# SSD decay differences of three heads: from a broadcast load and VectorE arithmetic to TensorE products of block-diagonal operands

## The chip, the cores and the metric

The kernel runs on one core of one Trainium2 chip. The metric is the device time of one execution in microseconds (us), lower is better. The engines are called as the profile calls them: PE is TensorE (matmul), PEld its weight load, DVE is VectorE, ACT is ScalarE, POOL is GpSimd, SP is SyncE, which only issues transfers here. ACT and POOL issue some transfers as well.

## The reference

The program is a two-layer backbone over 512 latent and 256 context tokens of 1024 channels. What the change touches is the chunked state-space mixer (SSD) of layer 0. It has 24 heads in 4 groups of 6, two directions, and chunks of 128 tokens: 6 chunks in all, 2 of them context.

```python
acs = jnp.cumsum(chunks(dt * a), axis=2)
seg = acs[:, :, :, None] - acs[:, :, None, :]
decay = jnp.exp(jnp.where(mask, seg, -jnp.inf))
cb = jnp.einsum('bclgn,bcsgn->bclsg', cm_c, bm_c)
y_diag = jnp.einsum('bclsgh,bcsghp->bclghp', cb[..., None] * decay, xdt)
```

For each chunk and head, `seg[l, s]` is the difference of two running sums, one at the token `l` that is written and one at the token `s` that is read. It is needed for both directions, where it is clamped so that the exponent is never positive.

## The kernel before, in words

The program is one long list of instructions, which a scheduler puts into an order for each engine ahead of time; each engine then runs its own list strictly in that order and waits on semaphores. A transfer also takes one of eight completion semaphores (DMAHW0 to DMAHW7) in turn for SP and ACT together, so a transfer whose semaphore is still in use waits for the one eight places earlier.

**Start (lines 596 to 628).** SP loads x and the modulation weights `mraw` (512 KB each, tiles reused), PE sums them (L580), and DVE copies the sum out (L587). Nothing of the first projections runs before that.

**Time steps (dt_stage, lines 659 to 711).** The running sums `acs` of 6 chunks x 48 head-directions are made on PE (L693), transposed (L707), copied to `at` by ACT (L709) and written by one transfer to the DRAM table `acd` (L710). Meanwhile the Fourier channels go on: `dft_channels` leaves its product in PSUM, ACT casts it to `ah` and DVE forms the rest `al` (L96, L97, shown as `ah`, `al`), and `dft_tokens` multiplies these on PE (L123).

**SSD (lines 796 to 1116).** For each of 4 groups, `ssd(G)` yields step by step, and between its steps the main loop emits filling work: `xbc_unit` (projection, a 5-tap convolution `co` on DVE at L855), `z_block`, and for the last group the output projection (`accumulate1`, L480). Splitting a weight into two parts takes ACT (L96) and DVE (L97). `decay(G, c, a)` is called 48 times, for 4 groups, 6 chunks and the two halves `a` of three heads. At the first half it forms `cb2` (L913, L915). Then SP loads `ab`, the sums of three heads in two directions broadcast to all 128 partitions (L918). DVE subtracts the sum at `s` (`nacs`) and clamps, three times for one direction (L924) and three times for the other, taking the minimum of both (L926). ACT and DVE form the weighted `w` (L923, L929), ACT takes the exponent (L932), POOL multiplies (L933), and `diag` uses the result one step later (L941).

The ring `ab` has two buffers, so the load of one call waits for the exponent of the call two before. PSUM has eight banks: four for `ps_mm` (ps1: the large products), two for `ps_s` (psum1: states, cb, transposes), one each for `ps_y` and `ps_off`.

Of the kernel before, what the change touches and what calls it, by code (L numbers as in the profile page):

```python
# [8 lines left out]
F32 = mybir.dt.float32  # L9
F32R = mybir.dt.float32r  # L10
# [16 lines left out]
FILL_LEAD = 1.0  # L27
LAMBDA_INIT = 0.8 - 0.6 * math.exp(-0.3)
# [27 lines left out]
def backbone_kernel(ctx, tc, xt, vec, dtrow, dskip, lam, w_mod, w_gate, w_up, w_down, w_in0, w_out0, w_in1, w_out1,  # L56
                    consts, dft_c, dft_l, rope, out):
# [88 lines left out]
    # ------------------------------------------------------------ modulation vectors  # L146
# [68 lines left out]
    def step_after(gen, n, after):  # L215
        """Steps of background work that no engine issues before the given instructions."""
        with ExitStack() as st:
            for i in after:
                st.enter_context(tc.issue_after(i))
            step(gen, n)  # L220
# [5 lines left out]
    # ------------------------------------------------------------ norms over channels  # L226
# [5 lines left out]
    def rsqrt(y, src, count):  # L232
        """1 / sqrt(src / count + eps): Newton's iteration from a guess that halves the exponent."""
# [84 lines left out]
    def gate(t, src, g):  # L318
        """The channels that GpSimd takes, scaled ahead of the rest"""
# [3 lines left out]
    def scale_both(t, src, g, r, a=0, b=KT):  # L323
        """t = src, scaled by channel and by token, from channel tile a to b; t holds the gated channels already"""
# [5 lines left out]
    def shift_split(t, m, xh, xl):  # L330
        """The two parts of t, shifted by channel"""
# [10 lines left out]
    def hasty(f):  # L342
        """Puts a stage of the turn before what is emitted ahead of it but doesn't wait for it."""
# [5 lines left out]
    class Turn:  # L349
        """Residual update of h by the mixer or FFN output o, then the next pre-norm, in stages per token block."""  # L350
# [32 lines left out]
        def last(self, b, psum1, between, out):  # L383
            """The whole update of the last block: nothing else is left to hide its steps."""
# [48 lines left out]
        def whole(self):  # L433
            """The pre-norm, put together again from its parts"""
# [5 lines left out]
    class Shift:  # L440
        """A tile of one token block, addressed by the tokens of the whole."""
# [7 lines left out]
    class Blocks:  # L449
        """Token blocks kept apart, addressed by the tokens of the whole."""  # L450
# [31 lines left out]
    # ------------------------------------------------------------ layer 0  # L482
# [5 lines left out]
    acd = dram.tile([6, 48, 128], F32, name="acd")  # L488
# [5 lines left out]
    nacs = sd.tile([128, 6, 48], F32, name="nacs")  # L494
# [8 lines left out]
    # time steps of the SSD and Fourier channels  # L503
    with ExitStack() as es:
# [38 lines left out]
        def scaled(b):  # L543
            """The pre-norm scaled, without its shift."""
# [114 lines left out]
        def dt_stage():  # L659
# [38 lines left out]
            nc.scalar.mul(nacs, acs, -1.0)  # L698
# [1267 lines left out]
```

## Time and profile before

| what | value |
|---|---|
| runs, us | 2404.7, 2405.3, 2398.96; median 2404.7 |
| span of the profiled execution, us | 2404.4 (the page gives no other time for it) |
| PE busy | 2123.5 us (88%) |
| DVE busy | 1951.7 us (81%) |
| ACT busy | 1124.8 us (47%) |
| POOL busy | 1187.3 us (49%) |
| mean granted PE clock | 0.934 of full speed |

Busy time counts the time from an instruction's start to its end; matmuls are pipelined, so a busy PE is not necessarily at its peak rate. The chain of waits is followed back from the last instruction: each step names what released it. A group of the trace's lines gives busy time and the mean of one, then the idle time of the engine before it and what ended that idle time.

### The profile page before, as it was taken

The page shows a single profiled execution, that of the slowest core. Times are in us where ns is not written, and L with a number is a line of the kernel's source. Part 1 is how long each engine was busy: PE and PEld are TensorE (multiplying, and loading weights), DVE is VectorE, ACT ScalarE, POOL GpSimd, SP SyncE. Part 2 cuts the span into 40 slices and gives each one's busy share as a digit, 9 for nine tenths or more (in the row PEclk, how much of TensorE's full clock was granted, in tenths as well). Part 3 has the DMA queues.
Part 4 walks back from the last instruction along what each step waited for, and adds up shares of the span by engine and source line. Part 5 has one row for each costly group of instructions (what it writes and reads, how often), then busy time and mean ns, then how long its engine had stood idle before and what let it go on. Part 6 is the DMA issues. An engine that isn't in the chain of part 4 may idle for free.

```text
span 2404.4 us, 33829 instructions
## 1 busy us (share of the span) xinstructions
PE 2123.5 (88%) x12594; PEld 1888.4 (79%) x12594; DVE 1951.7 (81%) x3035; ACT 1124.8 (47%) x1966; POOL 1187.3 (49%) x903
## 2 busy tenths in 40 slices
PE   7898989888987779899999987988889977999997
PEld 3787878776767678889999987766667776899997
DVE  4858987879897788998888878788778777888886
ACT  4535565646433344333333443654556643544443
POOL 1525656556543546664555543284842223555553
PEclk9999999999998689999999988998889987999998
DMA  7334332324430523333333321111101213222321
GB/s 257 132 130 137 124 112 81 129 89 147 139 113 7 165 100 110 114 114 132 120 118 133 124 97 53 44 44 36 42 29 40 75 44 114 79 106 98 105 97 53
DMA packets 90390, 239.43 MB, mean 100 GB/s; under 512 B 8433, under 2 KB 38289, under 8 KB 90225
## 3 DMA queue, kind: packets, MB, share of 16 engines
q1 hardware_dynamic: 71808, 214.95, 26.1%
q10 hardware_dynamic: 16944, 17.20, 2.2%
q0 software_dynamic: 1472, 5.11, 0.5%
q8 instruction: 99, 1.62, 0.3%
q14 instruction: 67, 0.54, 0.1%
HBM read 217.82 MB, written 18.37 MB: 98 GB/s over the span
## 4 chain that ended last, share of the span: by engine, by line
PE 41%; DVE 35%; issue 7%; DMA 7%; ACT 6%; POOL 4%; SPq 0%; ACTq 0%; POOLq 0%; DVEq 0%
PE ps_mm L123 33%; DVE w L97 6%; DMA mraw<-in_w_mod_dram 4%; DVE w L929 2%; DVE macc L175 2%; DVE co L855 2%; DMA ab<-acd 2%; DVE ab L924 2%; DVE ab L926 1%; PE ps_at L123 1%; DVE sx L1518 1%; DVE facc L326 1%; DVE mx L1629 1%; PE ps_s L580 1%; POOL wt L1184 1%
## 5 line engine op out<-in xcount | busy, mean ns | idle before, releaser
L123 PE MATMUL ps_mm<-xh,w 128*128 128x256 f32 (+2 forms) x3600 | 854.5, 331 | 55.6 <-DVE w L97 20.3
L123 PEld LDWEIGHTS ps_mm<-xh,w 128*128 128x128 f32 x3600 | 616.8, 197 | 108.3 <-DVE w L97 24.2
L123 PE MATMUL ps_mm<-xl,w 128*128 128x256 f32 (+2 forms) x1800 | 557.6, 329 | 8.6 <-DVE xl L338 3.5
L123 PE MATMUL ps_mm<-hid,w 128*128 128x384 f32 (+2 forms) x2244 | 408.0, 339 | 30.8 <-DVE facc L1371 11.9
L123 PEld LDWEIGHTS ps_mm<-hid,w 128*128 128x128 f32 x2244 | 367.5, 193 | 62.8 <-DVE facc L1371 17.6
L123 PEld LDWEIGHTS ps_mm<-xl,w 128*128 128x128 f32 x1800 | 339.1, 196 | 31.8 <-DVE xl L338 4.1
L97 DVE TENSOR_TENSOR w<-raw,w 128x512 fp32r<-128x512 f32 (+1 forms) x292 | 312.1, 1076 | 35.5 <-ACT w L96 34.3
L96 ACT CAST w<-raw 128x512 fp32r<-128x512 f32 (+1 forms) x323 | 236.9, 749 | 149.2 <-PE ps_mm L123 128.4
L180 POOL TENSOR_TENSOR macc<-macc,mraw 128x1024 f32<-128x1024 f32 x54 | 152.8, 2829 | 121.5 <-ACT mraw L179 118.0
L97 DVE TENSOR_TENSOR w<-wt,w 128x512 fp32r<-128x512 f32 x156 | 159.0, 1028 | 39.3 <-ACT w L96 39.2
L123 PE MATMUL ps_mm<-ys,w 128*128 128x256 f32 (+1 forms) x840 | 161.2, 348 | 22.1 <-ACT ys L96 8.9
L123 PEld LDWEIGHTS ps_mm<-ys,w 128*128 128x128 f32 x840 | 131.6, 201 | 43.9 <-DVE acc L480 12.3
L1184 POOL TENSOR_TENSOR wt<-raw 128x512 f32<-128x512 f32 x78 | 118.3, 1516 | 55.1 <-DMA raw<-in_w_up_dram 40.7
L96 ACT CAST w<-wt 128x512 fp32r<-128x512 f32 x156 | 93.4, 618 | 101.7 <-PE ps_mm L123 53.8
L1371 DVE TENSOR_TENSOR facc<-facc,ps_mm 128x384 f32<-128x384 f32 (+2 forms) x232 | 119.2, 557 | 21.1 <-PE ps_mm L123 20.9
L123 PE MATMUL ps_mm<-w,xh 128*128 128x256 f32 x576 | 118.6, 305 | 12.9 <-ACT cin L849 10.7
L97 POOL TENSOR_TENSOR w<-raw,w 128x1024 fp32r<-128x1024 f32 x31 | 81.1, 2615 | 82.5 <-ACT w L96 82.4
L175 DVE SCALAR_TENSOR_TENSOR macc<-mraw,silc,macc 128x1024 f32<-128x1024 f32 x54 | 98.3, 1820 | 27.4 <-DMA mraw<-in_w_mod_dram 27.2
L1184 POOL TENSOR_TENSOR wt<-raw,wt 128x512 f32<-128x512 f32 x39 | 64.6, 1656 | 104.0 <-DVE w L97 103.3
L123 PEld LDWEIGHTS ps_mm<-w,xh 128*128 128x128 f32 x576 | 96.1, 202 | 19.0 <-ACT cin L849 12.7
L179 ACT ACTIVATE mraw<-mraw,silc 128x1024 f32<-128x1024 f32 x54 | 62.1, 1152 | 84.4 <-DVE macc L175 35.8
L1516 POOL TENSOR_TENSOR sx<-sx 128x512 f32<-128x512 f32 x60 | 95.3, 1588 | 2.3
(405 smaller groups left out, 4273.7 us busy)
## 6 DMA issues: line engine op xcount, KB each, us to landing
mraw<-in_w_mod_dram SPq DMA_DIRECT2D x96, 512.0 KB, 4.2
raw<-in_w_in_dram SPq DMA_DIRECT2D x69, 512.0 KB, 3.4
raw<-in_w_gate_dram SPq DMA_DIRECT2D x44, 512.0 KB, 3.3
raw<-in_w_up_dram SPq DMA_DIRECT2D x44, 512.0 KB, 3.2
raw<-in_w_down_dram SPq DMA_DIRECT2D x44, 512.0 KB, 3.3
ab<-acd SPq DMA_DIRECT2D x48, 384.0 KB, 3.7
raw<-in_w_out_dram SPq DMA_DIRECT2D x32, 512.0 KB, 3.3
res<-rd ACTq DMA_DIRECT2D x5, 1024.0 KB, 8.7
```

The costliest lines, as they stand in the source:

```text
L96: nc.scalar.copy(hi, raw)
L97: (eng or nc.vector).tensor_tensor(out=lo, in0=raw, in1=f32(hi), op=SUB)
L123: last = nc.tensor.matmul(dst, a, b[:, sl], start=(start and i == 0), stop=(stop and i == 2))
L175: nc.vector.scalar_tensor_tensor(out=acc, in0=raw, scalar=s, in1=acc, op0=MUL, op1=ADD)
L179: nc.scalar.activation(raw, raw, AF.Identity, scale=s)
L180: nc.gpsimd.tensor_tensor(out=acc, in0=acc, in1=raw, op=ADD)
L855: nc.vector.scalar_tensor_tensor(out=co, in0=cin[:, j:j + CW], scalar=vcol(V_CW5 + ti * 5 + j), in1=co, op0=MUL, op1=ADD)
L924: nc.vector.tensor_scalar(out=ab[:, 0, h, :], in0=ab[:, 0, h, :], scalar1=nacs[:, c, r0 + h:r0 + h + 1], scalar2=0.0, op0=ADD, op1=ALU.min)
L929: nc.vector.scalar_tensor_tensor(out=w[:, h, :], in0=G.cb2[:, 1], scalar=dtt[:, c, r0 + 3 + h:r0 + 4 + h], in1=w[:, h, :], op0=MUL, op1=ADD)
L1184: nc.gpsimd.tensor_tensor(out=t, in0=a, in1=b, op=op)
L1371: nc.vector.tensor_tensor(out=acc[:, m, s], in0=acc[:, m, s], in1=ps, op=ADD)
L1516: nc.gpsimd.tensor_tensor(out=cv, in0=cv, in1=t, op=ADD)
```

## The change

The table `acd` gives way to `sgd`, one block of 24 rows by 896 columns for each chunk and each three heads. Rows 0 to 11 hold the sums along `l` in block-diagonal places (12 rows: high and low part of three heads in two directions) over a weight of -1; rows 12 to 23 hold ones in block-diagonal places over the sums along `s` as weights. The constant part comes from the input `segbg` by one DRAM-to-DRAM transfer with a broadcast source, issued on ACT at the start; the sums are written into it by 32 small transfers on ACT in `dt_stage`. In `decay`, SP loads one block into one of two fixed tiles `sg`, two PE products of 384 columns leave minus the difference of both directions in PSUM, ACT writes the positive part (Relu) to `ex`, DVE takes one maximum over 128x384, and ACT takes the exponent of the negative. The bank count goes from 4 and 2 to 3 and 3. Comments removed by the diff are left out here.

```diff
+SG_R, SG_N = 24, 896
...
-    acd = dram.tile([6, 48, 128], F32, name="acd")
+    sgd = dram.tile([6, 8, SG_R * SG_N], F32, name="sgd")
+    nc.scalar.dma_start(out=sgd.rearrange("c a n -> (c a) n"),
+                        in_=segbg.rearrange("r n -> (r n)").partition_broadcast(48))
...
-            nc.scalar.mul(nacs, acs, -1.0)
...
-            at = tp.tile([48, T], F32, tag="at", name="at")
-            nc.scalar.copy(at, pq[0:48, :])
-            nc.scalar.dma_start(out=acd.rearrange("c h t -> h c t"), in_=at.rearrange("h (c t) -> h c t", c=6))
+            at = [p.tile([48, T], F32R, tag=t, name="at", bufs=1) for p, t in ((tp, "at"), (fp, "yo"))]
+            split(pq[0:48, :], *at)
+            for i, p in enumerate(at):
+                p = f32(p)
+                for a in range(8):
+                    src = p[6 * a:6 * a + 6].rearrange("j (c t) -> j c t", c=6)
+                    r0 = 6 * i * SG_N
+                    nc.scalar.dma_start(
+                        out=sgd[:, a, r0:r0 + 6 * 1024].rearrange("c (j m) -> j c m", m=1024)[:, :, 0:128], in_=src)
+                    r0 = (12 + 6 * i) * SG_N
+                    nc.scalar.dma_start(
+                        out=sgd[:, a, r0:r0 + 6 * SG_N].rearrange("c (j m) -> j c m", m=SG_N)[:, :, 768:SG_N], in_=src)
...
         def ps1():
-            return psp.tile([128, 512], F32, tag="mm", name="ps_mm", bufs=4)
+            return psp.tile([128, 512], F32, tag="mm", name="ps_mm", bufs=3)
         def psum1():
-            return psp.tile([128, 512], F32, tag="s", name="ps_s", bufs=2)
+            return psp.tile([128, 512], F32, tag="s", name="ps_s", bufs=3)
...
-            ab = sq_.tile([128, 2, 3, 128], F32, tag="ab", name="ab", bufs=2)
-            nc.sync.dma_start(out=ab.rearrange("p d h l -> p (d h) l"),
-                              in_=acd[c, r0:r0 + 6, :].partition_broadcast(128))
+            sg = state["sg"][state["n"] % 2]
+            state["n"] += 1
+            nc.sync.dma_start(out=f32(sg[0:SG_R, :]), in_=sgd[c, 2 * g + a].rearrange("(r n) -> r n", n=SG_N))
+            pds = []
+            for d in range(2):
+                pd = psum1()[:, 0:GW]
+                nc.tensor.matmul(pd, sg[:, 768:SG_N], sg[:, d * GW:d * GW + GW], start=True, stop=True)
+                pds.append(pd.rearrange("p (h l) -> p h l", h=3))
+            ex = sq_.tile([128, 3, 128], F32, tag="ex", name="ex", bufs=3)
+            nc.scalar.activation(ex, pds[0], AF.Relu)
             w = sq_.tile([128, 3, 128], F32, tag="w", name="w", bufs=2)
-            ex = sq_.tile([128, 3, 128], F32, tag="ex", name="ex", bufs=3)
             for h in range(3):
                 nc.scalar.activation(w[:, h, :], G.cb2[:, 0], AF.Identity, scale=dtt[:, c, r0 + h:r0 + h + 1])
-                nc.vector.tensor_scalar(out=ab[:, 0, h, :], in0=ab[:, 0, h, :],
-                                        scalar1=nacs[:, c, r0 + h:r0 + h + 1], scalar2=0.0, op0=ADD, op1=ALU.min)
-                nc.vector.scalar_tensor_tensor(out=ab[:, 0, h, :], in0=ab[:, 1, h, :],
-                                               scalar=nacs[:, c, r0 + 3 + h:r0 + 4 + h], in1=ab[:, 0, h, :],
-                                               op0=ADD, op1=ALU.min)
                 nc.vector.scalar_tensor_tensor(out=w[:, h, :], in0=G.cb2[:, 1],
                                                scalar=dtt[:, c, r0 + 3 + h:r0 + 4 + h], in1=w[:, h, :],
                                                op0=MUL, op1=ADD)
-            nc.scalar.activation(ex, ab[:, 0], AF.Exp)
+            nc.vector.tensor_tensor(out=ex, in0=ex, in1=pds[1], op=ALU.max)
+            nc.scalar.activation(ex, ex, AF.Exp, scale=-1.0)
             nc.gpsimd.tensor_tensor(out=ex, in0=ex, in1=w, op=MUL)
...
-        state = {}
+        state = {"n": 0, "sg": [sq_.tile([128, SG_N], F32R, name="sg%d" % i) for i in range(2)]}
+        for sg in state["sg"]:
+            nc.gpsimd.memset(f32(sg), 0.0)
```

The change's own file has other line numbers: there the broadcast transfer is L490, the 32 transfers are L717 and L720, `cb2` is L926, the two products are L935, the Relu is L938, `w` on DVE is L942 and the maximum is L945.

The order of the instructions moves at three places. The first is SP at the start of the program: x, the modulation weights and the first weights of layer 0. The names in brackets are what a row waits for. Before:

```order
L75 DMA vecs<-in_vec_dram 128x445
L528 DMA x_111<-in_xt_dram 128x8x256
L576 DMA mraw<-in_w_mod_dram 128x1024 x3
L576 DMA mraw<-in_w_mod_dram 128x1024 [waits DMAHW0_49]
L576 DMA mraw<-in_w_mod_dram 128x1024 [waits DMAHW1_49]
L576 DMA mraw<-in_w_mod_dram 128x1024 [waits DMAHW4_49,DMAHW2_49,PE_49]
L107 DMA raw<-in_w_in_dram 128x1024 [waits DMAHW3_49]
```

And with the change:

```order
L76 DMA vecs<-in_vec_dram 128x445
L530 DMA x_111<-in_xt_dram 128x8x256
L578 DMA mraw<-in_w_mod_dram 128x1024 x2
L578 DMA mraw<-in_w_mod_dram 128x1024 [waits DMAHW0_49]
L578 DMA mraw<-in_w_mod_dram 128x1024 [waits DMAHW1_49]
L578 DMA mraw<-in_w_mod_dram 128x1024 [waits DMAHW2_49]
L578 DMA mraw<-in_w_mod_dram 128x1024 [waits DMAHW4_49,DMAHW3_49,PE_49]
```

The broadcast transfer on ACT has taken a completion semaphore. The other early transfers hold 0 (consts), 1 (vecs), 2 (x), 4 and 6 (mraw), 5 (dsk) and 7 (rows), so it holds DMAHW3, and the sixth `mraw` now waits for it.

The second place is ACT while the time steps end and the third Fourier group is cast (`ah`). Before, one transfer stands between the casts:

```order
L709 COPY at<-ps_mm 48x768 [waits PE_49]
L96 CAST ah<-ps_s 128x512 [waits PE_49,Activation_49]
L710 DMA acd<-at 48x6x128 [waits Activation_49]
L703 ACTIVATE tend<-tend 128x288 [waits DVE_49]
L96 CAST ah<-ps_s 128x512 [waits PE_49] x2
```

With the change 32 transfers stand there. The last ones and what follows them:

```order
L720 DMA sgd<-at 6x6x128 [waits DMAHW5_49]
L717 DMA sgd<-at 6x6x128 [waits DMAHW6_49]
L720 DMA sgd<-at 6x6x128 [waits DMAHW7_49]
L717 DMA sgd<-at 6x6x128 [waits DMAHW0_49]
L720 DMA sgd<-at 6x6x128 [waits DMAHW1_49]
L97 CAST ah<-ps_s 128x512 [waits PE_49] x2
```

The second and third cast of that group have moved behind all 32 transfers; PE's own order in this stretch is unchanged.

The third place is the decay itself in the first group of the SSD. On DVE, before, from the third `cb` on:

```order
L915 TENSOR_TENSOR cb_2498<-ps_s,cs 128x256 [waits PE_49]
L924 TENSOR_SCALAR ab<-ab,nacs 128x128 [waits DMAHW2_49,Activation_49]
L924 TENSOR_SCALAR ab<-ab,nacs 128x128
L855 SCALAR_TENSOR_TENSOR co<-cin,vecs,co 128x772 [waits DVE_49]
L924 TENSOR_SCALAR ab<-ab,nacs 128x128
L926 SCALAR_TENSOR_TENSOR ab<-ab,nacs 128x128 [waits DVE_49] x2
L929 SCALAR_TENSOR_TENSOR w<-cb_2498,dtt,w 128x128 [waits Activation_49]
```

On DVE with the change, from the same `cb` on:

```order
L926 TENSOR_TENSOR cb_2530<-ps_s,cs 128x256 [waits PE_49]
L942 SCALAR_TENSOR_TENSOR w<-cb_2530,dtt,w 128x128 [waits Activation_49] x6
L945 TENSOR_TENSOR ex<-ex,ps_s 128x384 [waits PE_49,Activation_49]
L971 TENSOR_TENSOR t<-ps_off,eac 128x192 [waits PE_49]
L971 TENSOR_TENSOR t<-ps_off,eac 128x192
```

On PE with the change, where one of the new products stands among those of a projection:

```order
L124 MATMUL ps_mm<-xh_74,w 128x256
L124 MATMUL ps_mm<-xl_75,w 128x512
L124 MATMUL ps_mm<-xl_75,w 128x256
L124 MATMUL ps_mm<-xh_74,w 128x512
L124 MATMUL ps_mm<-xh_74,w 128x256
L935 MATMUL ps_s<-sg_2112 128x384 [waits DMAHW2_49,DVE_49]
```

The load's wait has moved from DVE, where L924 had it, to PE, where L935 has it together with a wait for a free bank.

## Rows read from the trace of the kernel before

**Rows 1.** The page's head.

```profile
span 2404.4 us, 33829 instructions
```

**Rows 2.** Busy time and clock in the stretch 240 to 740 us (the SSD).

```profile
core 0: us, PE busy (x) PEld busy (x) DVE busy (x) ACT busy (x) POOL busy (x), PEclk, DMA share, GB/s
240.00:740.00 500.00, 447.34 (x2625) 382.01 (x2624) 422.12 (x830) 263.93 (x486) 281.01 (x347) 0.96 0.34 113
```

**Rows 3.** The chain of waits by line, 240 to 740 us.

```profile
by line: PE ps_mm L123 25.5%; DVE w L929 9.3%; DMA ab<-acd 7.9%; issue 7.6%; DVE ab L924 7.4%; DVE ab L926 6.3%; DVE co L855 5.1%; PE ps_s L894 3.6%; DVE w L97 3.2%; DVE bc L855 3.1%; DVE acc L480 2.6%; DVE t L957 2.6%; ACT L932 2.3%; DVE y
```

**Rows 4.** DVE's groups by line, 240 to 740 us.

```profile
L926 DVE SCALAR_TENSOR_TENSOR ab<-ab,nacs 128x128 f32<-128x128 f32 x144 | 61.8, 471 | 0.0
L924 DVE TENSOR_SCALAR ab<-ab,nacs 128x128 f32<-128x128 f32 x144 | 57.3, 447 | 38.9 <-DMA ab<-acd 37.4 <-ACT ex L932 1.4
L904 DVE TENSOR_TENSOR so<-so,ps_s 128x384 f32<-128x384 f32 x32 | 17.5, 546 | 14.8 <-POOL so L901 9.1 <-PE ps_s L894 5.5
```

**Rows 5.** Who waited for whom on PE and SP, 240 to 740 us: total, times, longest.

```profile
PE ps_s L979 <- DVE yg L976: 10.6, 5, 4.5
PE ps_mm L123 <- DVE acc L480: 8.9, 6, 2.6
PE ps_off L953 <- DVE t L957: 7.6, 5, 3.8
PE ps_mm L123 <- ACT cin L849: 4.8, 4, 2.2
...
SPq L918 <- ACT ex L932: 127.7, 34, 13.5
```

**Rows 6.** The timeline at the start: the sixth `mraw` and the first copy of the sums.

```profile
1.91 13.81 SPq L576 DMA_DIRECT2D mraw<-in_w_mod_dram  x6
...
29.04 0.67 DVE L587 COPY mrow<-ps_s 2x512 f32<-2x512 f32 x1
```

**Rows 7.** The start in three stretches, columns as in rows 2.

```profile
0.00:8.00 8.00, 0.00 (x0) 0.00 (x0) 0.24 (x2) 1.50 (x2) 0.20 (x4) 1.00 0.52 172
8.00:20.00 12.00, 8.21 (x20) 2.15 (x21) 2.24 (x4) 5.26 (x8) 0.00 (x0) 1.00 0.95 355
20.00:29.00 9.00, 9.00 (x24) 2.05 (x23) 5.03 (x3) 2.46 (x3) 3.11 (x1) 1.00 0.88 301
```

**Rows 8.** The chain of waits, 140 to 168 us.

```profile
141.81 5.37 PE ps_mm L123 x24
...
158.84 8.56 PE ps_mm L123 x47
```

**Rows 9.** One unbroken stretch of PE products in the chain of waits.

```profile
620.75 8.47 PE ps_mm L123 x48
```

**Rows 10.** PE's and ACT's groups of 384 columns and the table loads, 240 to 740 us.

```profile
L894 PE MATMUL ps_s<-xe,btok 128*128 128x384 f32 x80 | 32.4, 490 | 4.1 <-DVE yt L987 3.3 <-DVE so L904 0.6
...
L932 ACT ACT_TABLE_LOAD x24 | 30.8, 1283 | 14.8 <-issue 14.5
...
L897 ACT COPY so<-ps_s 128x384 f32<-128x384 f32 x8 | 3.8, 478 | 29.8 <-PE ps_s L894 29.8
```

**Rows 11.** Transfers: size and median us from issue to landing.

```profile
ab<-acd SPq DMA_DIRECT2D x48, 384.0 KB, 3.7
...
rd<-h_c SPq DMA_DIRECT2D x1, 1024.0 KB, 5.9
...
acd<-at ACTq DMA_DIRECT2D x1, 144.0 KB, 2.3
...
dsk<-in_dskip_dram ACTq DMA_DIRECT2D x1, 24.0 KB, 6.0
```

**Rows 12.** The timeline of ACT and of PE around 140 us.

```profile
139.49 0.35 ACTq L710 DMA_DIRECT2D acd<-at  x1
...
140.30 0.58 ACT L96 CAST ah<-ps_s 128x512 fp32r<-128x512 f32 x1
...
143.98 0.40 PE L123 MATMUL ps_mm<-dh,ah 128*128 128x512 f32 x1
```

More of the change, by code (lines that the diff above doesn't have):

```diff
@@ L56, in backbone_kernel @@
 def backbone_kernel(ctx, tc, xt, vec, dtrow, dskip, lam, w_mod, w_gate, w_up, w_down, w_in0, w_out0, w_in1, w_out1,
-                    consts, dft_c, dft_l, rope, out):
+                    consts, dft_c, dft_l, rope, segbg, out):
     nc = tc.nc
@@ L493, in backbone_kernel @@
     acs = sd.tile([128, 6, 48], F32, name="acs")
-    nacs = sd.tile([128, 6, 48], F32, name="nacs")
     eac = sd.tile([128, 6, 48], F32, name="eac")
@@ L1890, in _tables @@
     rope = np.stack([np.concatenate([cos, cos], 0), np.concatenate([sin, sin], 0)], 1).astype(f4)
-    return dict(consts=consts, dft_c=dft_c, dft_l=dft_l, rope=np.ascontiguousarray(rope))
+    segbg = np.zeros((24, 896), f4)
+    segbg[0:12, 768:] = -1
+    for j in range(12):
+        segbg[12 + j, (j % 6) * 128:(j % 6) * 128 + 128] = 1
+    return dict(consts=consts, dft_c=dft_c, dft_l=dft_l, rope=np.ascontiguousarray(rope), segbg=segbg)
 def _layout(inputs):
@@ L1940 @@
 _INS = ['xt', 'vec', 'dtrow', 'dskip', 'lam', 'w_mod', 'w_gate', 'w_up', 'w_down', 'w_in0', 'w_out0', 'w_in1', 'w_out1',
-        'consts', 'dft_c', 'dft_l', 'rope']
+        'consts', 'dft_c', 'dft_l', 'rope', 'segbg']
 def kernel(**inputs):
```

## The prediction

> **What bounds the kernel now.** I read the page's slices and the busy times by stretch first. Of a span of 2404.4 us [rows 1] the part that the change works in runs from about 240 to 740 us. There [rows 2] PE is busy 447 of 500 us and DVE 422, so neither alone fills the stretch. The reader should see two engines that take turns in holding each other up. The chain of waits for that stretch [rows 3] shows how: PE's large products are 25.5% of it, while what the change takes from DVE is 7.9% (the load of `ab`) + 7.4% (L924) + 6.3% (L926) = 21.6%, or 108 us. DVE's groups [rows 4] give the size: the two lines are busy 61.8 + 57.3 = 119 us, and DVE stood idle another 38.9 us ahead of L924, 37.4 of it for the load. PE's longest waits [rows 5] are for DVE: 10.6 + 8.9 + 7.6 = 27.1 us of the 31.9 in the four longest. SP [rows 5] waited 127.7 us to issue the load of `ab`, because the exponent of the call two before still held the buffer.
>
> PE's loss is the most that can be won. It is idle 500 - 447 = 53 us. Its mean granted clock is 0.96 of full, that is, 8% of the time at the lower level of 1.2 GHz, which loses 4% or 20 us. Together 73 us.
>
> The second thing to see is the start and the stretch around 140 us, where the change adds work. Both lie on the path: the first copy of the modulation sums comes at 29.04 us [rows 6], the transfers before that run at 0.95 and 0.88 of the engines' time [rows 7], and from 141.8 to 167.4 us the chain is nearly all PE products [rows 8].
>
> **The change part by part.** *DVE in the SSD.* Removed: 119 us busy and up to 39 us of waiting. Added: 48 maxima over 128x384 with one operand in PSUM, at the 546 ns of L904, which has that shape and an operand in PSUM [rows 4]: 26 us. DVE is thus needed 93 us less, and 132 us less counted with the waiting, out of 422 + 39 = 461. What is late next is PE itself.
>
> *PE in the SSD.* Added: 96 products of 384 columns. Nearest below is the unbroken stretch of 48 products in 8.47 us [rows 9]; these are 24 of 512 and 24 of 256 columns, so 18432 columns, 0.46 ns each, and 384 columns take 0.18 us. Above is the 490 ns row of a product as wide in the other number format [rows 10]. I take 0.18, since the new operands have the format of the stretch: 17 us, up to 47.
>
> How much of the 73 us PE gets back is my choice. DVE ends about 27 of 32 us of the longest waits, 0.85; DVE loses 132 of 461 us, so a queue in front of it that was nearly always full is now often empty, and I let 0.7 of those waits go: 0.85 x 0.7 = 0.6, or 44 us. Net of the products: **27 us less**. The ends are 0 (the new waits eat it) and 73 - 17 = 56.
>
> *ACT and the banks.* ACT gains 48 Relus at the 478 ns of a 384-column copy out of PSUM [rows 10], 23 us, and its order holds ten more table loads than before in this part, at 1283 ns [rows 10], 13 us. It is busy 264 of 500 us, so both are covered, as long as nothing waits for a Relu: it frees a bank for PE. The large products lose one of four banks; the two waits that this ring shows, for `acc` 8.9 us and `cin` 4.8 [rows 5], are what could double, 14 us at most. I take nothing, and keep this for the slow case. One removed ACT copy (`nacs`) and the two fills of `sg` on POOL, once each, move nothing.
>
> *Loads in the SSD.* 86 KB in place of 384 KB, between the 2.3 us of 144 KB and the 3.7 us of `ab` [rows 11]. They wait for PE two calls before, not for the exponent, so SP's 127.7 us of standing still go, and the weights queued behind on SP come no later.
>
> *Start.* 48 blocks of 24 x 896 x 4 bytes are 4.13 MB, read and written in DRAM. From 8 to 20 us 0.95 of the engines moved 355 GB/s [rows 7], so 374 at full, and the copy takes 11.0 us of all engines. Free until 29 us are 0.48 x 8 + 0.05 x 12 + 0.12 x 9 = 5.5 us [rows 7]. Lower end: 11.0 - 5.5 = 5.5 us. Upper end by the nearest row that writes DRAM, 1.05 MB in 5.9 us [rows 11]: 23 us, less 5.5, so 17.5. SP's sixth `mraw`, issued at about 15.3 us [rows 6], now waits for the whole copy, so the delay can't be put off; I take **8 us more**, nearer to the lower end, since one large copy pays a landing time once. What follows shifts as it is.
>
> *Time steps.* 32 issues on ACT in a row at 0.35 us [rows 12] are 11.2 us; SP is not touched. The second cast, which ran at 140.30, starts at 151.5 and ends at 152.1. PE needs it for the product that it started at 143.98 [rows 12]: it stands for **8 us**. If each eight issues had to wait for a landing of 3.7 us [rows 11] (semaphores go round by eight), it would be 14.8 - 11.2 = 3.6 more. Ends 7 and 12. The further split on DVE lies in DVE's idle time there.
>
> **Sum.** 2404.4 - 27 + 8 + 8 = 2393.4 against the profiled execution's span; the median of the runs is 2404.7, so 0.3 us apart, and I forecast **2393**.
>
> **A rule weighed.** The row of `dsk` shows a 24 KB transfer on ACT's queue landing after 6.0 us while SP's large loads move, against 2.3 us for 144 KB later [rows 11], so queues slow each other. The Trainium skill, "DMA: Bandwidth & Descriptors", section "Queues, rings and completion order", says that each DMA engine changes between queues only after a whole packet of descriptors; the row agrees with sharing and says nothing on what is drained first. By the row's sharing the start costs 8 us as above; by the rule the copy could pass ahead whole and cost 11 us or more, which is a rival below.
>
> **The rivals.** *Slower: the wait moves from DVE to PE.* The 96 products stand in PE's own order between those of the projections, each behind a free bank (read by a Relu or a maximum) and the first of a pair behind the load, which on SP stands behind stores and weights. If PE pays half of DVE's 37.4 us [rows 4], the time is 2393 + 19 = 2412; with all of it and the lost bank, 2393 + 37 + 14 = 2444. It is slower by over 0.3% from 0.2 us per product on. For it: PE has no way around a wait, and ACT's Relu queues behind casts and table loads. Against it: the load goes out two calls ahead.
>
> *No difference: DVE was not what held PE.* PE gets back 30 of the 73 us: 2404.4 - 13 + 16 = 2407. For it: 25.5% of the chain is PE's own products [rows 3].
>
> *The copy goes ahead whole* and costs up to the upper end: 2404.4 - 27 + 11 + 8 = 2396 to 2402. For it: SP waits for its end.
>
> *Much faster: PE gets all back*, and the start costs its low ends: 2404.4 - 56 + 5.5 + 7 = 2361. Against it: the 27 us at most that rows show as waits for DVE.
>
> That the change doesn't do what it says I exclude: the order shows one maximum where six operations stood.
>
> **How the numbers follow.** A measurement tells 0.3%, 7.2 us, from no change: faster is below 2397.5, slower above 2411.9. Forecast 0.42, its own range 2380 to 2400: 0.38 faster, 0.04 same. Slower rival 0.19, all slower. No difference 0.20: 0.16 same, 0.04 slower. The whole copy 0.08: 0.03 faster, 0.05 same. Much faster 0.11. Sums: faster 0.52, same 0.25, slower 0.23. The range 2366 to 2418 leaves out about half of the much faster case and two thirds of the slower one, 0.18.
>
> **What would show it.** In the changed profile the first copy of the sums should come at about 37 us, not 29.04; PE should stand about 8 us for `ah` near 152 us (plus the shift), with 32 issues on ACT. In the SSD DVE should be about 93 us less busy, the maximum take 0.55 us, and the new products 17 us of PE time; the stretch should be 27 us shorter. PE's waits for DVE should be well below 27 us. The forecast is wrong if the new products wait over 0.2 us each, or if the start is late by over 15 us.

## The result and the profile after

The changed kernel takes 2419.4 us (median of 4 runs, 2413.6 to 2421.7) against 2403.2 for the kernel before, a ratio of 1.0068 (95% interval 1.0053 to 1.0083): 16 us **slower**. The forecast was 2393, and 2419.4 lies just outside its range. The profiled execution's span is 2419.9 us, 15.5 more than [rows 1]. Of all runs below one, among five of the products issued twice, took 5805.2 us where the other four lie between 2414.1 and 2430.5, and is left out.

The part that the change is meant for did become faster. The first table row below is the kernel before, the second the changed one; each entry is the start, in us, of one landmark in the trace: the first modulation sum on PE (L580 before), the first projection product (L123), the first running sum of the time steps (L693), the last copy of `yo` (L765), the first copy of `cin` (L849), the first state of the SSD (L894), the last transposes of `yg` (L979), and the span.

| profile | sum | projection | running sum | `yo` | `cin` | states | `yg` | span |
|---|---|---|---|---|---|---|---|---|
| before | 11.8 | 35.5 | 133.0 | 158.5 | 167.4 | 254.8 | 770.3 | 2404.4 |
| after | 29.5 | 52.9 | 155.3 | 190.4 | 199.3 | 294.7 | 785.9 | 2419.9 |
| difference | 17.7 | 17.4 | 22.3 | 31.9 | 31.9 | 39.9 | 15.6 | 15.5 |

Read along the last row, the time is lost in four steps and won back in one: **+17.4** at the start, +4.9 up to the running sums, **+9.6** in the time steps, **+8.0** from `cin` to the first states, **-24.3** in the SSD. From `yg` to the end nothing is left over (1634.1 and 1634.0 us).

*Start.* The chain of waits of the changed kernel from 0 to 52 us, its three longest pieces:

```profile
1.20 21.17 DMA x<-in_xt_dram
...
29.56 6.44 PE ps_s L582 x12
...
36.87 9.46 DMA x<-in_xt_dram
```

The load of x, which SP issues at 1.20 us, ends 21 us later. The three stretches of [rows 7], and SP's sixth `mraw` of [rows 6], in the changed kernel:

```profile
0.00:8.00 8.00, 0.00 (x0) 0.00 (x0) 0.06 (x1) 1.50 (x2) 0.20 (x4) 1.00 0.82 276
8.00:20.00 12.00, 0.00 (x0) 0.00 (x0) 0.00 (x0) 0.00 (x0) 0.00 (x0) 1.00 0.92 295
20.00:29.00 9.00, 2.53 (x11) 2.44 (x12) 2.24 (x4) 3.73 (x6) 0.00 (x0) 1.00 0.74 298
```

```profile
1.91 31.00 SPq L578 DMA_DIRECT2D mraw<-in_w_mod_dram  x6
```

From 8 to 20 us no engine computes anything, while the transfers run at 0.92 of the engines' time and 295 GB/s. The sixth `mraw` went out at 32.59 us. What it waited for last was PE, 8.9 us for sums that read the tile, and not the copy, which landed at 20.3 us in the run below that adds it alone. PE's own timeline shows a second thing:

```profile
25.92 1.87 PE L259 MATMUL ps_mm<-cs,sq 128*128 128x1 f32 x8 [25.92 <-DVE sq L285]
28.34 1.22 PE L271 MATMUL ps_mm<-cs,nq 128*128 128x128 f32 x4 [0.55 <-DVE nq L265]
29.49 15.08 PE L582 MATMUL ps_s<-mraw,silc 128*2 128x512 f32 x32
```

In the kernel before, the sums of the first two of the eight weights ran first (8 of 32 records, two to a product), and the norm of x stood between the sums:

```profile
11.79 5.78 PE L580 MATMUL ps_s<-mraw,silc 128*2 128x512 f32 x8 [11.79 <-DMA mraw<-in_w_mod_dram]
17.50 1.05 PE L258 MATMUL ps_mm<-cs,sq 128*128 128x1 f32 x8
18.48 5.31 PE L580 MATMUL ps_s<-mraw,silc 128*2 128x512 f32 x12
```

Now the norm stands ahead of all 32, so the sums wait for x and its norm as well as for their weights.

*Time steps.* ACT's timeline, the first and last of the 32 issues, the cast behind them and the last `yo`:

```profile
161.65 0.54 ACTq L717 DMA_DIRECT2D sgd<-at  x1
...
172.93 0.32 ACTq L720 DMA_DIRECT2D sgd<-at  x1
173.29 1.07 ACT L97 CAST ah<-ps_s 128x512 fp32r<-128x512 f32 x2 [10.60 <-DMA sgd<-at]
...
190.37 0.80 ACT L776 COPY yo<-ps_mm 128x768 f32<-128x768 f32 x1 [6.22 <-PE ps_mm L124]
```

The issues hold ACT for 11.6 us, and the cast stands behind them as forecast. PE's wait for it, from the first running sum to the last `yo`:

```profile
PE ps_mm L124 <- ACT ah L97: 7.6, 1, 7.6
```

The rest of the 9.6 us goes with the clock: 0.81 of full speed is granted in this stage against 0.93 before, so more of it runs at the lower of the two levels, 1.2 GHz, and PE is busy 27.5 us in place of 25.3.

*SSD.* Busy time, clock and transfers from the first state to the last transposes, columns as in [rows 2]; the kernel before, then the changed one:

```profile
254.80:771.50 516.70, 459.66 (x2718) 393.56 (x2716) 429.51 (x846) 270.01 (x499) 288.36 (x346) 0.95 0.32 105
```

```profile
294.70:787.00 492.30, 465.36 (x2814) 400.20 (x2812) 351.66 (x611) 303.33 (x557) 295.25 (x347) 0.98 0.26 81
```

PE's idle time falls from 57.0 to 26.9 us and its granted clock rises from 0.95 to 0.98. DVE is busy 78 us less. The new products and the maximum, by line:

```profile
L935 PE MATMUL ps_s<-sg x96: 331/338/637, 316.0 to 718.6; 128*128 128x384 f32 x96
```

```profile
L945 DVE TENSOR_TENSOR ex<-ex,ps_s x48: 536/542/556, 317.9 to 721.8; 128x384 f32<-128x384 f32 x48
```

The 96 products waited 1.3 us in all, and PE's waits for DVE in that stretch are short (the wait for `acc` of [rows 5] is 3.8 us now, not 8.9):

```profile
PE ps_s L993 <- DVE yg L990: 6.0, 3, 2.7
PE ps_y L955 <- POOL ex L947: 5.8, 8, 2.2
PE ps_mm L124 <- DVE acc L481: 3.8, 8, 1.3
```

So the wait did not move from DVE to PE. SP still stands for the two `sg` tiles, 105.5 us where it stood 127.7 for `ab` [rows 5], without holding up PE:

```profile
SPq L931 <- PE ps_s L935: 105.5, 34, 11.9
```

The last product on PE that uses a decay (L941 before, L955 now) starts at 726.1 instead of 746.3 us, but after it comes more of the output projection than before, 59.8 us to the last transposes in place of 24.0. The chain there is for the most part PE's large products (82.9% from 726 to 786 us), in its two longest pieces:

```profile
726.40 11.16 PE ps_mm L124 x63
739.43 19.59 PE ps_mm L124 x111
```

### The profile page after: what moved, and what is told of

Read it like the earlier page. It is cut to its first block, busy times and chain, and to the rows that moved or that the text cites. A ratio compares the mean times of both kernels' runs of the same rounds, so it can differ in the third digit from the quotient of the medians.

```text
span 2419.9 us, 33896 instructions
## 1 busy us (share of the span) xinstructions
PE 2137.3 (88%) x12690; PEld 1904.3 (79%) x12690; DVE 1878.0 (78%) x2796; ACT 1159.6 (48%) x2024; POOL 1186.3 (49%) x905
## 4 chain that ended last, share of the span: by engine, by line
PE 48%; DVE 26%; issue 8%; ACT 7%; DMA 5%; POOL 5%; ACTq 0%; SPq 0%; POOLq 0%; DVEq 0%
PE ps_mm L124 38%; DVE w L98 5%; DMA mraw<-in_w_mod_dram 3%; DVE macc L176 2%; PE ps_at L124 1%; DMA x<-in_xt_dram 1%; DVE co L866 1%; ACT w L97 1%; DVE mx L1645 1%; DVE sx L1534 1%; PE ps_s L582 1%; PE ps_s L905 1%; DVE facc L327 1%; POOL macc L181 1%; DVE w L942 1%
## 5 line engine op out<-in xcount | busy, mean ns | idle before, releaser
L124 PE MATMUL ps_mm<-xl,w 128*128 128x256 f32 (+2 forms) x1800 | 558.1, 327 | 10.1 <-DVE xl L339 5.5
L98 DVE TENSOR_TENSOR w<-wt,w 128x512 fp32r<-128x512 f32 x156 | 153.1, 991 | 39.5 <-ACT w L97 39.3
L124 PE MATMUL ps_mm<-ys,w 128*128 128x256 f32 (+1 forms) x840 | 154.9, 338 | 18.6 <-ACT ys L97 8.0
L124 PEld LDWEIGHTS ps_mm<-ys,w 128*128 128x128 f32 x840 | 126.2, 196 | 39.2 <-ACT ys L97 8.9
L124 PE MATMUL ps_mm<-w,xh 128*128 128x256 f32 x576 | 113.6, 295 | 3.4 <-ACT cin L861 1.7
```

The lines of the kernel that those rows point to most:

```text
L98: (eng or nc.vector).tensor_tensor(out=lo, in0=raw, in1=f32(hi), op=SUB)
L124: last = nc.tensor.matmul(dst, a, b[:, sl], start=(start and i == 0), stop=(stop and i == 2))
```

## The experiments

The theory (A) was that the change's own gain is there and that the loss is its preparation: the copy at the start, the 32 issues on ACT, and a stage ahead of the SSD that lost a bank. The rivals (B) were that the products themselves cost it, or that each loss would only move elsewhere. All times are medians and ratios to the kernel before on the same chip. Different programs differ by some microseconds where their code is the same: from the last `yg` transposes to the end the thirteen profiles lie between 1626.6 and 1640.8 us, and from the first sum to the first running sum, where five of them have the same order on PE, these took 121.0 (writes on SP), 123.1 (banks 4 and 2), 123.2 (copy alone), 125.8 (the changed kernel) and 126.6 us (products twice). So each experiment is read at its landmarks first.

| profile | sum | projection | running sum | `yo` | `cin` | states | `yg` | span | ratio (95%) |
|---|---|---|---|---|---|---|---|---|---|
| copy late | 11.5 | 35.4 | 140.7 | 174.4 | 183.3 | 278.6 | 770.0 | 2396.6 | 0.9990 (0.9979 to 1.0001) |
| copy alone | 28.6 | 52.8 | 151.8 | 175.8 | 184.8 | 272.1 | 787.7 | 2415.4 | 1.0068 (1.0052 to 1.0084) |
| writes on SP | 31.2 | 54.9 | 152.2 | 177.6 | 185.2 | 276.2 | 765.9 | 2402.6 | 0.9998 (0.9983 to 1.0012) |
| banks 4 and 2 | 29.7 | 53.1 | 152.8 | 186.4 | 195.3 | 282.7 | 780.2 | 2409.9 | 1.0023 (1.0012 to 1.0033) |
| flat layout | 11.5 | 35.7 | 133.2 | 158.7 | 167.6 | 262.5 | 753.8 | 2391.6 | 0.9964 (0.9952 to 0.9977) |
| flat, two pools | 11.5 | 36.3 | 135.6 | 159.9 | 169.1 | 255.1 | 744.9 | 2375.6 | 0.9887 (0.9867 to 0.9906) |
| products twice | 29.9 | 53.7 | 156.5 | 191.6 | 200.5 | 295.6 | 796.0 | 2428.7 | 1.0085 (1.0057 to 1.0114) |
| half copy alone | 23.3 | 47.0 | 146.2 | 170.2 | 178.7 | 265.8 | 782.3 | 2415.9 | 1.0055 (1.0034 to 1.0076) |
| copy, order held | 24.4 | 49.0 | 149.2 | 173.2 | 182.1 | 269.3 | 788.4 | 2429.2 | 1.0096 (1.0081 to 1.0110) |
| norm first | 17.0 | 41.2 | 141.8 | 165.8 | 174.8 | 262.1 | 778.2 | 2416.4 | 1.0058 (1.0043 to 1.0074) |
| before, two pools | 11.9 | 36.9 | 134.9 | 160.3 | 169.5 | 260.0 | 778.9 | 2409.7 | 1.0016 (1.0004 to 1.0028) |

**The copy later.**

```diff
-    nc.scalar.dma_start(out=sgd.rearrange("c a n -> (c a) n"),
-                        in_=segbg.rearrange("r n -> (r n)").partition_broadcast(48))
...
         after = list(turned)
+        with ExitStack() as st:
+            for i in after:
+                st.enter_context(tc.issue_after(i))
+            nc.scalar.dma_start(out=sgd.rearrange("c a n -> (c a) n"),
+                                in_=segbg.rearrange("r n -> (r n)").partition_broadcast(48))
```

> The changed kernel, but the 4.13 MB copy that fills the table is not issued at the program's start: ACT's queue issues it after the last shift of the first pre-norm (about 100 us later), still before the 32 small writes. Theory A (the start loss is the copy's traffic ahead of x and the first modulation weights, 18.7 us in the two traces): the first modulation product goes back from 29.5 to about 12 us, the first projection from 54.2 to 36, and the time from 2419.4 to 2401, plus 0 to 3 us for the copy at its new place beside the modulation loads, so 2401 to 2405. Rival B (the loss belongs to the products and their order, and a late start is caught up or lost anyway): the first projection goes back but the end does not, 2414 to 2420.

2402.8 us (2397.5 to 2406.2), as A expects. The first projection is back at 35.4. At the running sums it is 7.7 us late (140.7 against 133.0). The changed kernel loses 4.9 there with no copy beside it, so the price at the new place is between 2.9 and 7.7 us, where 0 to 3 were expected: the copy is issued at 73.75 us, and the chain then has one load of modulation weights that takes 12.5 us beside it.

```profile
81.55 12.53 DMA mraw<-in_w_mod_dram
```

**The copy alone.**

```diff
+    sgd = dram.tile([48, 24 * 896], F32, name="sgd")
+    nc.scalar.dma_start(out=sgd, in_=w_in0[0].rearrange("r n -> (r n)")[0:24 * 896].partition_broadcast(48))
```

> The kernel before with nothing but a copy of the same size and shape (48 times 84 KB, from a weight tensor into a DRAM tile that nobody reads), issued at the same place on ACT's queue; nothing of the result changes. Theory A: the start loses 17 to 20 us and all of it reaches the end, 2403.2 + 18.7 = 2422 (2419 to 2425). Rival B (most of the copy is hidden, and the changed kernel starts late for another reason, such as the order of the norm ahead of the modulation products): 2404 to 2411.

2422.7 us (2417.2 to 2427.2): A again. A copy that nobody reads makes the kernel before 17.3 us late at the first projection, and still 17.3 at the first states and at `yg`. Nothing up to there absorbs it. Transfers from 0 to 29 us, with the time from issue to landing last; this kernel, then the kernel before:

```profile
sgd<-in_w_in_dram ACTq DMA_DIRECT2D x1, 4032.0 KB, 19.1
mraw<-in_w_mod_dram SPq DMA_DIRECT2D x5, 512.0 KB, 21.2
x<-in_xt_dram SPq DMA_DIRECT2D x1, 1024.0 KB, 20.3
```

```profile
mraw<-in_w_mod_dram SPq DMA_DIRECT2D x12, 512.0 KB, 10.2
x<-in_xt_dram SPq DMA_DIRECT2D x3, 1024.0 KB, 9.0
```

The copy and x are issued together, at 1.20 us on two queues, and land together, so a load a quarter of the size takes as long as the copy. The two queues of the changed kernel from 8 to 17 us show how (packets, MB, share of the engines' time; q10 is ACT's queue, with the copy, and q1 is SP's):

```profile
q10 hardware_dynamic: 68, 2.80, 91.9%
q1 hardware_dynamic: 70, 0.11, 4.7%
```

The Trainium skill, "DMA: Bandwidth & Descriptors", section "Queues, rings and completion order", has the engines take packets from the queues in turn; 68 packets of one queue beside 70 of the other agree with that. But a packet of the copy has 41 KB on average and one of SP's queue 1.6 KB, so in these 9 us the copy moves 25 times as much as x and the weights: it passes almost whole ahead of the rest of x.

**Half the copy.** As above with 24 blocks in place of 48.

> The kernel before with half of the copy that was tried alone: 24 blocks of 84 KB. Theory A (the whole copy is paid at the rate that the start's transfers reach, about 4.2 us for each MB, with nothing free): half of it costs half, 8 to 9 us in the marks after the start, about 2414. Rival B (as the prediction priced it: some 5.5 us of transfer time at the start are free, the rest is paid): (17.4 + 5.5) / 2 - 5.5 = 6 us by the rate measured, or 0 by the rate forecast: 2406 to 2412.

2415.5 us (2409.5 to 2423.5). Neither theory fits the landmarks: half the copy costs 11.5 us at the first projection and the whole 17.3. So 5.8 us go with each half, 11.6 for the whole, and 5.7 do not depend on the size. That the norm stands ahead of the sums in both was the obvious candidate.

**The order held, and the order alone.** The first puts the norm's products (in `rstd_stages`, between the two pieces of the diff) behind the sums of the fourth weight, beside the whole copy (not quite the old order: the kernel before has them behind the second weight's); the second has no copy and puts all sums behind the norm.

```diff
+        if pin and count == 1024:
+            hold = tc.issue_after(pin.pop())
+            hold.__enter__()
...
+        if hold is not None:
+            hold.__exit__(None, None, None)
...
-            mod_sum(mps, raw, k)
-            if k in (1, 4, 5):
+            m = mod_sum(mps, raw, k)
+            if k == 3:
+                pin.append(m)
+            if k in (3, 4, 5):
                 step(nx)
```

```diff
+        step(nx)
+        step(nx)
         for k in range(KT):
             raw, lead = mod_raw(1, k)
-            mod_sum(mps, raw, k)
-            if k in (1, 4, 5):
+            with tc.issue_after(fence[0]):
+                mod_sum(mps, raw, k)
+            if k == 5:
                 step(nx)
```

> The kernel before with the whole copy alone at the start, as tried first (17.4 us late, 2422.7), but with the first norm's products on PE held behind the sums of the first four modulation weights, as they stood in the kernel before; with the copy the order had them ahead of all sixteen sums. Half a copy cost 11.4 us and the whole 17.4, so 6 us for each half and 5.4 that don't scale. Theory A (the 5.4 us are that order: PE waits for x and its norm with weights already there): the first sum comes about 5 us earlier than 28.6, the first projection and all after it too, and the time is 2404 + 12 to 13 = 2416 to 2418. Rival B (the sums wait for their own transfers, which share with the copy, whatever the order): first projection at 54 us and 2420 to 2424.

> The kernel before without any copy, but with the sixteen modulation sums on PE held behind the first norm's products, as the order stands with the copy. Theory A (the order costs 5 us by itself): first sum at about 16.5 us in place of 11.8, first projection at 40 to 41 in place of 35.5, 2408 to 2410. Rival B (without the copy the sums catch up, since they are paced by the loads of their weights): first projection within 1.5 us of 35.5, 2402 to 2406.

The order alone makes the first projection 5.7 us late (41.2), as much as the part that didn't scale: the sums free their tiles later, and the second load of x, which SP issues behind the next `mraw`, goes out at 25.02 us in place of 21.24. With the copy and the order held the first sum comes 4.3 us earlier than with the copy alone, and the first projection 3.8. It is then still 13.5 us late, where the copy's own share was put at 11.6, so 1.9 us stay open. PE's timeline, copy with the order held, then the order alone:

```profile
24.36 8.57 PE L590 MATMUL ps_s<-mraw,silc 128*2 128x512 f32 x16 [24.36 <-DMA mraw<-in_w_mod_dram]
32.86 1.05 PE L264 MATMUL ps_mm<-cs,sq 128*128 128x1 f32 x8
```

```profile
13.44 1.86 PE L258 MATMUL ps_mm<-cs,sq 128*128 128x1 f32 x8 [13.44 <-DVE sq L284]
15.85 1.22 PE L270 MATMUL ps_mm<-cs,nq 128*128 128x128 f32 x4 [0.55 <-DVE nq L264]
17.00 15.71 PE L580 MATMUL ps_s<-mraw,silc 128*2 128x512 f32 x32
```

Theory A therefore holds in the main at the start, but its times were missed: 2429.0 us (2425.7 to 2431.0) where 2416 to 2418 were expected, and 2417.3 (2413.7 to 2427.6) where 2408 to 2410 were. The first is level with the copy alone by `yg` (788.4 and 787.7) and 13 us behind it after that, in code that neither edit touches but whose order is drawn up anew for each program. Why it came out worse was not followed up.

**The small writes on SP.**

```diff
-                    nc.scalar.dma_start(
+                    nc.sync.dma_start(
```

(both calls under `for a in range(8)`)

> The changed kernel with the 32 small writes of the decay sums issued by SP in place of ACT. Theory A (ACT's 11.6 us of issues hold the casts that the token transform waits for, 9.8 us in the two traces): the last copy of that stage goes from 190.4 to about 181 and the time to 2419.4 - 9 = 2410, 2409 to 2413 with what the issues cost SP's own loads. Rival B (the writes hold whichever queue carries them: SP's weight loads for the stage after stand behind 11.6 us of issues): 2416 to 2421, with the loss then in the first projections of the SSD part.

2405.0 us (2395.9 to 2411.8): more than A expects. From the running sum to the last `yo` it takes 25.4 us, as in the kernel before (25.5), where the changed kernel takes 35.1. SP issues the 32 writes from 157.21 to 168.62 us and its weights come in time, so B falls. The stage from `cin` to the first states is 91.0 us here, 4.4 shorter than in the changed kernel, which no edit explains.

**Banks four and two.**

```diff
-            return psp.tile([128, 512], F32, tag="mm", name="ps_mm", bufs=3)
+            return psp.tile([128, 512], F32, tag="mm", name="ps_mm", bufs=4)
...
-            return psp.tile([128, 512], F32, tag="s", name="ps_s", bufs=3)
+            return psp.tile([128, 512], F32, tag="s", name="ps_s", bufs=2)
```

> The changed kernel with the PSUM banks of the SSD part as before: four for the projections and two for the small tiles, in place of three and three. Theory A (the 8 us that the changed kernel loses between the first transposes and the first states come from the fourth projection bank): that stage goes back from 78.5 to about 70.5 us; in the SSD the two decay products then stand in the only two banks and wait for VectorE's maximum to free them, some 0.5 to 1 us for each of 48 steps of which the projections beside them hide half, so +12 and -8: about 2423 (2411 to 2435). Rival B (those 8 us come from elsewhere, the later start and the loads that it meets): the stage stays at 77 to 80 us, and the time is 2420 to 2440.

2410.3 us (2406.9 to 2417.1), faster than the changed kernel and just below A's range. From `cin` to the first states it is 87.4 us, exactly that of the kernel before, against 95.4 with three banks (70.5 from the first transposes, as A has it): the 8 us are the bank. The other profiles bear it out: the six with four banks take 87.1 to 87.4 us here, of the five with three banks four take 94.9 to 95.4 and one, the writes on SP, 91.0. PE's waits there, changed kernel and then this one:

```profile
PE ps_mm L877 <- ACT cin L860: 8.9, 3, 4.7
PE ps_mm L124 <- DVE w L98: 4.3, 2, 2.9
```

```profile
PE ps_mm L124 <- DVE w L98: 5.8, 2, 3.6
PE ps_mm L124 <- ACT cin L860: 5.7, 3, 4.3
```

With three banks the transposes (L877) stand 8.9 us until ACT's copy to `cin` has emptied one. In all PE stands 4.9 us longer in the stage than with four, and is busy 3.1 us longer, at a granted clock of 0.93 against 0.96. In the SSD the third small bank is worth less than I expected: 497.5 us with two, 491.2 with three.

**The products twice.**

```diff
-                nc.tensor.matmul(pd, sg[:, 768:SG_N], sg[:, d * GW:d * GW + GW], start=True, stop=True)
+                for _ in range(2):
+                    nc.tensor.matmul(pd, sg[:, 768:SG_N], sg[:, d * GW:d * GW + GW], start=True, stop=True)
```

> The changed kernel with each of the 96 decay products issued twice into the same bank (the second overwrites the first, the result is the same). It asks whether PE sets the length of the SSD part after the change. One product takes 338 ns in the profile, so 96 more are 32 us. Theory A (PE is the bound there now): 2419.4 + 26 to 34 = 2445 to 2453. Rival B (PE has idle time in which products cost nothing): 2420 to 2432.

The ratio is 1.0085 (1.0057 to 1.0114; median of four runs 2427.3 us), and the SSD part grows from 491.2 to 500.4 us. That is far below A's 26 to 34 and within B's range, but B's reason, products that cost nothing, doesn't hold, and A's price was wrong: the window from the first state to the last transposes shows

```profile
295.60:798.00 502.40, 478.47 (x2910) 418.93 (x2908) 349.25 (x611) 307.00 (x559) 288.99 (x347) 0.98 0.25 80
```

so 96 more products add 13.1 us to PE's busy time, 0.14 us each, although each is listed with 338 ns. Of those 13.1 us the window pays 10.1: most of what is added to PE lengthens the stage, and the second product of a pair costs less than half of its listed duration.

**No copy and no small writes: a flat layout.** Rows of column values need no zeros: the two rows over the weight -1 hold all six of a step one after the other.

```diff
+SG_R, SG_N = 14, 896
+    sgd = dram.tile([2, 6, 48, 128], F32, name="sgd")
+    sgb = dram.tile([SG_R, SG_N], F32, name="sgb")
...
+                nc.scalar.dma_start(out=sgd[i].rearrange("c h t -> h c t"), in_=f32(p).rearrange("h (c t) -> h c t", c=6))
...
+            nc.sync.dma_start(out=f32(sg[0:2, 0:768]), in_=sgd[:, c, r0:r0 + 6, :].rearrange("i j t -> i (j t)"))
+            for i in range(2):
+                nc.sync.dma_start(out=f32(sg[2 + 6 * i:8 + 6 * i, 768:SG_N]), in_=sgd[i, c, r0:r0 + 6, :])
...
+            nc.sync.dma_start(out=f32(sg[0:SG_R, :]), in_=sgb)
```

> The changed kernel with another layout of the decay operand: the six column values of a step stand one after the other in two rows (high and low part) of 768 columns over rows of -1, so no zeros are needed, the constant rows are loaded once into the two SBUF tiles, and the 4.13 MB copy goes; the 32 small writes become two. A step then loads 6 + 6 KB in three transfers in place of 84 KB in one. Theory A (the change's losses are the copy, 17 us, and the writes on ACT, 9 us, and the SSD part keeps its gain): 2419.4 - 17 - 9 = 2393, 2389 to 2397. Rival B (the three transfers of a step land later or fill SP, and PE stands before the products): the part from the first states to the last transposes is 500 us or longer in place of 491, and the time 2402 or more.

2393.8 us (2391.5 to 2396.7), as A expects. Every landmark up to `cin` is within 0.3 us of the kernel before, the stage before the states still takes 7.5 us more with three banks (94.9 us), and the SSD takes 491.3 us, so three small transfers a step hold nothing up.

**Flat, and two pools.**

```diff
-        psp = pool(es, "ps", 1, PSUM)
+        esp = ExitStack()
+        psp, nmm = pool(esp, "ps0", 1, PSUM), 5
...
+        esp.close()
+        psp, nmm = pool(es, "ps", 1, PSUM), 3
```

(`ps1` takes `bufs=nmm`)

> The layout of the run before, and two PSUM pools one after the other: five banks for the projections and three small ones until the SSD begins, then three and three as in the changed kernel. Theory A (the 8 us ahead of the first states are the missing fourth projection bank; the SSD needs the third small one): the stage from the first convolution input to the first states is 87 us in place of 95, the SSD stays at 491, and the time is 2393 - 8 = 2385, 2381 to 2389. Rival B (the border between the pools stops PE until the last banks are read, and costs what the bank gives): 2391 to 2396.

**2375.4 us** (2373.0 to 2377.5), ratio 0.9887: this version beats both kernels. The stage before the states is 86.0 us. Of the 18.4 us against the flat layout the landmarks show 7.4 at the first states and 8.9 at `yg`; the rest lies behind `yg` (1630.7 against 1637.8 us), within the spread named above. At the border between the pools (240 to 275 us) PE's only listed wait is 0.7 us, so it stops nothing. PE works as in the changed kernel:

```profile
255.10:746.00 490.90, 462.76 (x2813) 398.67 (x2812) 354.38 (x612) 304.08 (x557) 295.24 (x348) 0.98 0.23 75
```

**The two pools without the change.** The kernel before with five and three banks, then four and two.

> The kernel before with the two PSUM pools alone: five banks for the projections and three small ones until the SSD begins, then four and two as before. It asks how much of the fastest version's 26.7 us belongs to the banks and not to the decay on PE. Theory A (the fourth bank was enough; the fifth gives 1.4 us, the difference of that stage in the two profiles, 87.4 to 86.0): 2402 to 2405. Rival B (the banks give it whatever the decay does, as from the flat layout's 2393.8 to 2375.4): 2385 to 2393.

2408.4 us (2403.4 to 2412.9), ratio 1.0016: no gain, slightly outside A's range on the slow side. The stage ahead of the states takes 90.5 us with five banks here, 87.4 with four, so the fifth bank did not pay. So the banks are not what makes the fastest version fast; they only remove a loss that the change had brought.

## Why the prediction was wrong

The sum was 2404.4 - 27 + 8 + 8. Its terms, in the order of the prediction:

- *SSD, -27: right.* The stretch is 24.3 us shorter. The two halves stand too: PE got back 30.1 us of idle time and 16.0 of clock (0.05 x 516.7 - 0.02 x 492.3; 13.7 with the shares unrounded), 44 to 46 against the forecast 44, which rested on a chosen share of 0.6 and so is in part luck. Less the 24.4 us that the stretch lost, 19 to 22 are left for the products. They were taken at 17 us from the rate of an unbroken stretch [rows 9], and the doubled products give 13.1, so 6 us or more of it stay open. The listed duration, 338 ns each or 32 us, would have been the wrong price, as the expectation of that run shows.
- *DVE, maximum, Relu, loads:* 542 ns for the maximum against 546; DVE busy 78 us less rather than 93; no wait of PE came in their place. That SP's 127.7 us of standing still would go was wrong: 105.5 are left, but PE did not wait for these loads. The slower rival is refuted: the products waited 1.3 us, not 19.
- *Time steps, +8: right in kind, 9.6.* The row of 32 issues took 11.6 us, forecast 11.2, and PE stood 7.6 us for the cast behind it. What the sum left out is the clock, 0.81 there against 0.93. The writes on SP bring the 9.6 back.
- *Start, +8: the step that failed most.* It came to 17.4 at the first projection, at its own upper end of 17.5. The copy's 11.0 us were nearly right (11.6, by the half and the whole), but three sentences failed. "Free until 29 us are ... 5.5 us": with the copy 4.7 us still stand unused there (0.18 x 8 + 0.08 x 12 + 0.26 x 9), so almost nothing of it was won; from 8 to 17 us SP's queue moved 0.11 MB beside the copy's 2.80, and nothing runs until x is there. "SP's sixth `mraw` ... now waits for the whole copy": it waited for PE's sums until 32.6 us, when the copy had long landed. "What follows shifts as it is": the order of PE changed as well, with the norm ahead of the sums, and that alone costs 5.7 us.
- *Banks, taken at nothing: the second step that failed.* "The large products lose one of four banks; ... I take nothing." I looked for the waits in the SSD, where this was right. But `ps1` serves the stage ahead of the SSD as well, and that stage lost 8.0 us, which four banks give back.
- *Between projection and running sums, 4.9 us* were not foreseen. With the same order on PE that part took 97.3 (writes on SP), 99.0 (copy alone), 99.7 (banks 4 and 2) and 102.8 us (products twice) in other profiles, 102.4 here and 97.5 before. The spread between executions can make all of it; the granted clock, 0.92 here and 0.94 before, goes the same way. The cause stays open.

With 17.4 for the start and 8 for the bank the same sum would have been 2404.4 - 27 + 17.4 + 8 + 8 = 2410.8; the 4.9 us, the 1.6 more of the time steps and the smaller gain make the rest. The rival with the copy ahead whole, to which I gave 0.08, was the nearest: the queues took turns by packet, but with packets so unequal the copy passed almost whole. Its price is right by luck: 17.5 was an upper end from another row, and the 17.3 us of the copy alone are 11.6 for the copy and 5.7 for the order.

## What to carry to other kernels

A faster inner stage can be eaten by its preparation: price the setup at the place where it runs, and at a start where every transfer is waited for a copy costs its full size. When a table needs zeros or many small writes, look for a layout that doesn't: two flat rows replaced 4.13 MB and 32 writes, and the fastest version came from there. A bank that is taken away is paid in every stage that shares the pool, so read the waits in all of them; two pools one after the other stopped nothing at their border here. Whether a copy cut into smaller packets, or issued on SP's queue behind x, would let x through was not tried.

## What was not expected of the hardware

- Two transfers issued together on two queues, 4.13 MB and 1 MB, landed within 1.2 us of each other (19.1 and 20.3 us); without the larger one the smaller took 9.0. The two queues moved as many packets, but in 9 us 2.80 MB against 0.11.
- Products of 384 columns listed with 338 ns raised PE's busy time by 0.14 us each when they were doubled.
- The changed kernel's transfers, most of them the copy's, ran from 8 to 20 us at 0.92 of the transfer engines' time and 295 GB/s, where the loads of the kernel before made 355 GB/s at 0.95 [rows 7].
